# Row means of a 64 MiB tensor: 14-row loads with a shared last part, issued by GpSimd from the third load on

## The chip, the cores and the metric

One core of a Trainium2 chip. The metric is the time of one execution in microseconds (us) on the device; most executions of a kernel agree within 0.3%. All runs compared here were in the fast state, with a granted clock of 1.0. Ratios are the mean time of one kernel's fast runs over the mean of the other's fast runs of the same rounds, so they are not quite the ratios of the medians quoted beside them. The experiments ran in four batches, each on another chip; the kernel before took 164.75, 164.77, 164.87 and 164.93 us there (medians), so a difference of 0.2 us between batches means little.

Words used below: a "row" is 128 x 1024 floats, one row of 1024 for each of the 128 partitions, 0.5 MiB. A load "lands" when its semaphore tells the engines that its data is there. Loads are counted from 0. In the profile DVE is VectorE, ACT is ScalarE, POOL is GpSimd and SP is SyncE; a "packet" is one of its DMA records, here one partition's part of a load.

## The reference

```python
# x: (32, 512, 1024) float32, divisor: 1024.0
def reference(x, divisor):
    return (np.sum(x, axis=-1) / divisor).astype(np.float32)
```

There are 16,384 sums of 1024 numbers. The kernel gives each partition 128 of them, so x is 128 "rows" in the sense above, and all of it is read once.

## The kernel before

SyncE issues every load. VectorE sums the first five rows of a load of eight, ScalarE (ACT) the other three, and the pool has five buffers, so five loads can be under way.

```python
    bulk = [8] * 15
    tail = [4, 2, 1]
    pool = ctx.enter_context(tc.tile_pool(name="bulk", bufs=5))
    # ... (one-off tiles; one PSUM tile that takes ACT's unused output)
    def act_sum(dst, src):
        n = src.shape[-1]
        nc.scalar.activation(junk[:, :n], src, COPY, accum_out=dst)

    def sums(t, j, rows, for_act):
        d = rows - for_act
        if d:
            nc.vector.reduce_sum(out=res[:, j : j + d], in_=t[:, :d, :], axis=AX)
        for r in range(d, rows):
            act_sum(res[:, j + r : j + r + 1], t[:, r, :])

    j = 0
    for rows in bulk:
        t = pool.tile([P, 8, D], F32, name="t")
        nc.sync.dma_start(out=t[:, :rows, :], in_=xr[:, j : j + rows, :])
        sums(t, j, rows, rows * 3 // 8)
        j += rows
    # ... (the tail: loads of 4, 2 and 1 rows; then the last row in three pieces,
    #      two sums of it on VectorE and one on ACT, a sum of the three, two scalings)
    nc.sync.dma_start(out=out_v, in_=res)
```

## Time and profile before

| | before |
|---|---|
| time, median | 164.75 us (164.66 to 164.75, 3 runs) |
| span of the profiled run | 162.9 us |
| DMA engines | at 90% or more in all slices but the first and the last |
| one load of 8 rows | lands every 9.71 us, 432 GB/s |
| VectorE, ACT busy | 53%, 36% |

How to read it: the bytes set the time (the prediction has the sum). An engine's idle time costs nothing here. What can cost something is a moment in which no load is waiting for the DMA engines. The lines of the profile that carry this stand in the prediction.

### The profile page before, as it was taken

The numbers are of one execution on the slowest core, as the hardware profiler recorded it, in microseconds if no ns is written. First come the engines' busy times: TensorE is split into PE (matmuls) and PEld (weight loads), VectorE is DVE, ScalarE is ACT, GpSimd is POOL, SyncE is SP. The second block draws the span as 40 slices with busy tenths as digits, with TensorE's granted clock in tenths as the row PEclk, the third lists the DMA queues.
The fourth block names the chain that finished last, engine by engine and source line by source line (L and its number), as shares of the span: only waits on it lengthen the run. The fifth ranks groups of instructions, "written<-read, shape, count | busy, mean of one in ns | idle before, by whom it ended". The sixth has DMA issues, their size and how long they took to land.

```text
span 162.9 us, 222 instructions
## 1 busy us (share of the span) xinstructions
DVE 87.1 (53%) x22; ACT 58.1 (36%) x101; POOL 0.2 (0%) x4
## 2 busy tenths in 40 slices
DVE  0007639094571917549093672908448092763983
ACT  3006135080531607034080622608043070613692
POOL 0000000000000000000000000000000000000000
DMA  6999999999999999999999999999999999999990
GB/s 209 426 418 443 435 435 435 418 443 435 410 459 426 402 467 435 394 459 435 426 443 418 435 437 418 443 435 410 443 443 402 459 443 410 443 435 398 408 352 16
DMA packets 3169, 67.18 MB, mean 412 GB/s; under 512 B 352, under 2 KB 736, under 8 KB 992
## 3 DMA queue, kind: packets, MB, share of 16 engines
q1 hardware_dynamic: 3168, 67.18, 96.5%
q14 instruction: 1, 0.01, 0.0%
HBM read 67.11 MB, written 0.07 MB: 412 GB/s over the span
## 4 chain that ended last, share of the span: by engine, by line
DMA 90%; DVE 7%; issue 1%; SPq 0%; DVEq 0%
DMA t<-in_x_dram 61%; DMA last<-in_x_dram 30%; DVE res L53 7%; DVE part L77 0%; DVE res L76 0%; DVE part L78 0%; DVE res L79 0%; SPq L60 0%; DVE part L74 0%; DVEq L78 0%
## 5 line engine op out<-in xcount | busy, mean ns | idle before, releaser
L53 DVE TENSOR_REDUCE res<-t 128x5 f32<-128x5120 f32 x15 | 82.3, 5488 | 72.5 <-DMA t<-in_x_dram 72.5
L48 ACT ACTIVATE junk<-t 128x1024 f32<-128x1024 f32 x45 | 46.2, 1027 | 99.2 <-DMA t<-in_x_dram 98.3
L48 ACT ACTIVATION_READ_ACCUMULATOR junk<-t 128x1 f32 x45 | 8.4, 186 | 0.0
L48 ACT ACTIVATE junk<-tail 128x1024 f32<-128x1024 f32 x4 | 4.1, 1028 | 1.7 <-DMA tail<-in_x_dram 1.7
L53 DVE TENSOR_REDUCE res<-tail 128x2 f32<-128x2048 f32 (+1 forms) x2 | 3.4, 1743 | 0.0
L48 ACT ACT_TABLE_LOAD x1 | 1.3, 1283 | 0.7 <-PEq L97 0.7
L74 DVE TENSOR_REDUCE part<-last 128x1 f32<-128x512 f32 x1 | 0.7, 685 | 0.6 <-DMA last<-in_x_dram 0.6
L48 ACT ACTIVATION_READ_ACCUMULATOR junk<-tail 128x1 f32 x4 | 0.7, 186 | 0.0
L77 DVE TENSOR_REDUCE part<-last 128x1 f32<-128x256 f32 x1 | 0.4, 411 | 0.0
L48 ACT ACTIVATE junk<-last 128x256 f32<-128x256 f32 x1 | 0.4, 388 | 0.0
L76 DVE TENSOR_SCALAR res<-res 128x127 f32<-128x127 f32 x1 | 0.2, 216 | 0.0
L78 DVE TENSOR_REDUCE part<-part 128x1 f32<-128x3 f32 x1 | 0.2, 155 | 0.1
L48 ACT ACTIVATION_READ_ACCUMULATOR junk<-last 128x1 f32 x1 | 0.2, 187 | 0.0
L79 DVE TENSOR_SCALAR res<-part 128x1 f32<-128x1 f32 x1 | 0.2, 154 | 0.0
L97 POOL MEMSET const-uint8-127<- 128x1 uint8 x1 | 0.1, 102 | 0.0
L97 POOL MEMSET const-bfloat16-1.0<- 128x1 bf16 x1 | 0.1, 101 | 0.0
L97 POOL MEMSET const-float32-0.0<- 128x1 f32 x1 | 0.1, 98 | 0.2 <-issue 0.2
L97 POOL MEMSET const-float32-1.0<- 128x1 f32 x1 | 0.1, 98 | 0.0
## 6 DMA issues: line engine op xcount, KB each, us to landing
t<-in_x_dram SPq DMA_DIRECT2D x15, 4096.0 KB, 43.0
tail<-in_x_dram SPq DMA_DIRECT2D x1, 2048.0 KB, 47.5
tail<-in_x_dram SPq DMA_DIRECT2D x1, 1024.0 KB, 49.5
tail<-in_x_dram SPq DMA_DIRECT2D x1, 512.0 KB, 50.4
last<-in_x_dram SPq DMA_DIRECT2D x1, 256.0 KB, 48.2
last<-in_x_dram SPq DMA_DIRECT2D x2, 128.0 KB, 34.1
out_dram<-res SPq DMA_DIRECT2D x1, 64.0 KB, 1.5
```

Of the source, the lines that this page charges most:

```text
L48: nc.scalar.activation(junk[:, :n], src, COPY, accum_out=dst)
L53: nc.vector.reduce_sum(out=res[:, j : j + d], in_=t[:, :d, :], axis=AX)
L74: nc.vector.reduce_sum(out=part[:, 0:1], in_=last[:, 0:h], axis=AX)
L76: nc.vector.tensor_scalar_mul(out=res[:, :j], in0=res[:, :j], scalar1=scale)
L77: nc.vector.reduce_sum(out=part[:, 2:3], in_=last[:, h + q : D], axis=AX)
L78: nc.vector.reduce_sum(out=part[:, 3:4], in_=part[:, 0:3], axis=AX)
L79: nc.vector.tensor_scalar_mul(out=res[:, j : j + 1], in0=part[:, 3:4], scalar1=scale)
L97: nc = _bacc.Bacc("TRN2", target_bir_lowering=False, num_devices=1)
```

## The change

Its intent: fewer and larger loads, a shorter end, and loads issued by GpSimd, which has nothing else to do. From the third load on they go through the software descriptor generator, on a queue of their own; loads 0 and 1 stay on SyncE's hardware queue. Three buffers of 14 rows take the place of five of 8. Two smaller edits are left out of the cut below: ACT's unused output gets four PSUM tiles in place of one, and ACT's sums of a load are written ahead of VectorE's.

```diff
-    bulk = [8] * 15
-    tail = [4, 2, 1]
-    pool = ctx.enter_context(tc.tile_pool(name="bulk", bufs=5))
+    bulk = [14] * 8 + [8]
+    split = {14: 6, 8: 4, 4: 2, 2: 1}          # rows for ACT
+    tail = [4, 2]
+    pool = ctx.enter_context(tc.tile_pool(name="bulk", bufs=3))
     ...
-    for rows in bulk:
-        t = pool.tile([P, 8, D], F32, name="t")
-        nc.sync.dma_start(out=t[:, :rows, :], in_=xr[:, j : j + rows, :])
-        sums(t, j, rows, rows * 3 // 8)
+    for i, rows in enumerate(bulk):
+        t = pool.tile([P, 14, D], F32, name="t")
+        tc.keep_in_program_order((nc.sync if i < 2 else nc.gpsimd).dma_start(out=t[:, :rows, :], in_=xr[:, j : j + rows, :]))
+        sums(t, j, rows)
     ...                                          # tail, row and last: nc.gpsimd too
-    (the last row in three pieces, three partial sums, their sum, a scaling)
+    (the last two rows each as 704 + 320 columns, one part on VectorE and one on ACT;
+     one tensor_scalar adds the two parts and scales them)
```

More of the change, by code (lines that the diff above doesn't have):

```diff
@@ L33 @@
     out_v = out.tensor.reshape((P, J)).ap()
-    bulk = [8] * 15
-    tail = [4, 2, 1]
-    assert sum(bulk) + sum(tail) + 1 == J
-    pool = ctx.enter_context(tc.tile_pool(name="bulk", bufs=5))
+    bulk = [14] * 8 + [8]
+    split = {14: 6, 8: 4, 4: 2, 2: 1}
+    tail = [4, 2]
+    assert sum(bulk) + sum(tail) + 2 == J
+    pool = ctx.enter_context(tc.tile_pool(name="bulk", bufs=3))
     one = ctx.enter_context(tc.tile_pool(name="one", bufs=1))
-    psum = ctx.enter_context(tc.tile_pool(name="junk", bufs=1, space=bass.MemoryType.PSUM))
+    psum = ctx.enter_context(tc.tile_pool(name="junk", bufs=4, space=bass.MemoryType.PSUM))
@@ L42, with sums @@
     res = one.tile([P, J], F32, name="res")
     part = one.tile([P, 4], F32, name="part")
-    junk = psum.tile([P, D], F32, name="junk")
     def act_sum(dst, src):
         n = src.shape[-1]
+        junk = psum.tile([P, D], F32, name="junk")
         nc.scalar.activation(junk[:, :n], src, COPY, accum_out=dst)
-    def sums(t, j, rows, for_act):
-        d = rows - for_act
-        if d:
-            nc.vector.reduce_sum(out=res[:, j : j + d], in_=t[:, :d, :], axis=AX)
+    def sums(t, j, rows):
+        d = rows - split[rows]
@@ L54, in sums @@
         for r in range(d, rows):
             act_sum(res[:, j + r : j + r + 1], t[:, r, :])
+        nc.vector.reduce_sum(out=res[:, j : j + d], in_=t[:, :d, :], axis=AX)
     j = 0
-    for rows in bulk:
-        t = pool.tile([P, 8, D], F32, name="t")
-        nc.sync.dma_start(out=t[:, :rows, :], in_=xr[:, j : j + rows, :])
-        sums(t, j, rows, rows * 3 // 8)
+    for i, rows in enumerate(bulk):
+        t = pool.tile([P, 14, D], F32, name="t")
+        tc.keep_in_program_order((nc.sync if i < 2 else nc.gpsimd).dma_start(out=t[:, :rows, :], in_=xr[:, j : j + rows, :]))
+        sums(t, j, rows)
@@ L62 @@
         j += rows
-    for k, rows in enumerate(tail):
-        t = one.tile([P, rows, D], F32, name=f"tail{k}")
-        nc.sync.dma_start(out=t, in_=xr[:, j : j + rows, :])
-        sums(t, j, rows, (rows + 1) // 2)
+    for i, rows in enumerate(tail):
+        t = one.tile([P, rows, D], F32, name=f"tail{i}")
+        tc.keep_in_program_order(nc.gpsimd.dma_start(out=t, in_=xr[:, j : j + rows, :]))
+        sums(t, j, rows)
         j += rows
-    h, q = D // 2, D // 4
-    last = one.tile([P, D], F32, name="last")
@@ L72 @@
-    for a, b in ((0, h), (h, h + q), (h + q, D)):
-        nc.sync.dma_start(out=last[:, a:b], in_=xr[:, j, a:b])
-    nc.vector.reduce_sum(out=part[:, 0:1], in_=last[:, 0:h], axis=AX)
-    act_sum(part[:, 1:2], last[:, h : h + q])
-    nc.vector.tensor_scalar_mul(out=res[:, :j], in0=res[:, :j], scalar1=scale)
-    nc.vector.reduce_sum(out=part[:, 2:3], in_=last[:, h + q : D], axis=AX)
-    nc.vector.reduce_sum(out=part[:, 3:4], in_=part[:, 0:3], axis=AX)
-    nc.vector.tensor_scalar_mul(out=res[:, j : j + 1], in0=part[:, 3:4], scalar1=scale)
@@ L80 @@
-    nc.sync.dma_start(out=out_v, in_=res)
+    c = 704
+    t = one.tile([P, D], F32, name="row")
+    tc.keep_in_program_order(nc.gpsimd.dma_start(out=t, in_=xr[:, j, :]))
+    act_sum(part[:, 0:1], t[:, c:])
+    nc.vector.reduce_sum(out=part[:, 1:2], in_=t[:, :c], axis=AX)
+    nc.vector.tensor_scalar(
+        out=res[:, j : j + 1], in0=part[:, 1:2], scalar1=part[:, 0:1], scalar2=scale, op0=ADD, op1=MULT
+    )
+    nc.vector.tensor_scalar_mul(out=res[:, :j], in0=res[:, :j], scalar1=scale)
@@ new lines @@
+    j += 1
+    t = one.tile([P, D], F32, name="last")
+    tc.keep_in_program_order(nc.gpsimd.dma_start(out=t[:, :c], in_=xr[:, j, :c]))
+    tc.keep_in_program_order(nc.gpsimd.dma_start(out=t[:, c:], in_=xr[:, j, c:]))
+    act_sum(part[:, 2:3], t[:, :c])
+    nc.vector.reduce_sum(out=part[:, 3:4], in_=t[:, c:], axis=AX)
+    nc.vector.tensor_scalar(
+        out=res[:, j : j + 1], in0=part[:, 3:4], scalar1=part[:, 2:3], scalar2=scale, op0=ADD, op1=MULT
+    )
+    tc.keep_in_program_order(nc.sync.dma_start(out=out_v, in_=res))
```

## The prediction

> **What bounds the kernel now.** I read the engines' busy shares first, then the slices, the DMA queues, the chain that ended last, and last the timeline. Shares and slices of the kernel before:
>
> ```profile
> DVE 87.1 (53%) x22; ACT 58.1 (36%) x101; POOL 0.2 (0%) x4
> ...
> DMA  6999999999999999999999999999999999999990
> ...
> q1 hardware_dynamic: 3168, 67.18, 96.5%
> ```
>
> No computing engine is busy for much over half of the span; the DMA engines are at 90% or more in every slice but the first and the last, and one queue does it all for 96.5% of 16 engines' time. The chain (share of the span by what was waited for) says the same:
>
> ```profile
> DMA t<-in_x_dram 61%; DMA last<-in_x_dram 30%; DVE res L53 7%; DVE part L77 0%; DVE res L76 0%; DVE part L78 0%; DVE res L79 0%; SPq L60 0%; DVE part L74 0%; DVEq L78 0%
> ```
>
> 90% is transfers. The 7% of VectorE is where the chain hops from a late-issued load to the reduction that freed its buffer, while other loads were flowing: no idle DMA lies there, as the slices show. The stream's rate is in the timeline (start us, us, what; in brackets the idle time before it):
>
> ```profile
> 100.79 5.49 DVE L53 TENSOR_REDUCE res<-t 128x5 f32<-128x5120 f32 x1 [4.22 <-DMA t<-in_x_dram]
> ...
> 110.50 5.49 DVE L53 TENSOR_REDUCE res<-t 128x5 f32<-128x5120 f32 x1 [4.22 <-DMA t<-in_x_dram]
> ...
> 149.36 5.49 DVE L53 TENSOR_REDUCE res<-t 128x5 f32<-128x5120 f32 x1 [4.22 <-DMA t<-in_x_dram]
> ```
>
> Five loads of 4 MiB land between 100.79 and 149.36, so one takes 9.71 us: 432 GB/s, or 1.214 us a row (a "row" is 128 x 1024 floats, 0.5 MiB). The first load landed at 13.36, which is 3.65 more than its own 9.71. All 128 rows then land by 3.65 + 128 x 1.214 = 159.1; the last piece was issued at 129.9 and landed 29.4 later, at 159.3. So the whole time is the stream, 3.65 in front of it, and what follows it: the last arithmetic ended at 160.34, 1.0 after the landing, then the store and the end, to 162.9 (164.75 as timed).
>
> The first slice is 4.07 us at 209 GB/s, 0.85 MB or 2.0 us of stream. So bytes flow from about 2.1, and some 1.55 of the 3.65 pass between a load's last byte and its semaphore.
>
> **What the Trainium skill says.** (1) "DMA: Bandwidth & Descriptors", Where 436 GB/s comes from: the ports give 435.2 GB/s. The trace agrees, at 432; no way of issuing can gain more than 1% of the stream. (2) The same page, SWDGE vs HWDGE vs iDMA: software and hardware generators feed different queues inside each DMA engine, and the engine takes turns between them. The trace before has one data queue and can't show this; my range depends on it. (3) The same page, Latency and other measured facts: the first byte takes about 1 us on the software path against about 0.6 us. No software load is in this trace. (4) "SBUF — State Buffer", Who interferes with whom: a VectorE reduction never locks GpSimd out on this chip, a tensor_scalar can. The reductions of t are 82.3 us of VectorE here, the tensor_scalars 0.4 us and at the end, when all loads have been issued. So I count no starving of the generator.
>
> **The change part by part.**
>
> *Fewer, larger loads.* Before: 15 loads of 8 rows; after: 8 of 14 and one of 8. If the difference between 9.71 and the 9.64 us that 4 MiB take at the skill's 435.2 GB/s is a cost per load (estimate), six fewer loads, and some fewer small pieces, save about 0.5 us. It is on the path.
>
> *Tail.* Before, 1.0 us of arithmetic followed the landing of the last piece: a reduction (0.41), a sum of three partials (0.155), a scaling (0.154), with waits. After: a 320-wide reduction (between 411 ns for 256 and 685 for 512: 0.48) beside a 704-wide ACT sum started on the earlier piece, and one tensor_scalar (0.15). About 0.75. Saves 0.3.
>
> *More ACT work.* A row costs ACT 1.18 us (starts at 13.38, 14.56, 15.74), VectorE 1.07 ((5488 - 2277)/3). A 14-row load gives ACT 6 x 1.18 = 7.1 us and VectorE 8.70 (5488 + 3 x 1070), and it takes 14 x 1.214 = 17.0 us to arrive. Both stay well ahead: hidden.
>
> *Issuing on GpSimd.* 12 issues, of 1 to 2 us each by (3) (estimate), on an idle engine. The 15 SP issues were no cost either. What counts is only whether a load is in flight when each is issued.
>
> Base, if the DMA engines never run dry: 164.75 - 0.5 - 0.3 = 164.0 us.
>
> *Depth.* Before, five buffers; after, three of 14 rows. In order, a load is issued when the third one back has been consumed, so two loads (34 us) remain: enough, if loads complete in order. **They may not.** Loads 0 and 1 are on the hardware queue, load 2 is the first of the software queue, and its buffer is free, so it goes out at once, beside load 0. Its bytes come before load 1's, but the engines consume load 1 before load 2, and loads 4 and 5 wait for those two.
>
> With equal turns: loads 0 and 2 share the engines from 2.1 to about 36. Load 0 lands at some 36.7, is consumed at 45.4, load 3 has its first byte at 46.9 (1.5 later, estimate). Load 1, alone from 36.1, has 6.2 us left, which shared take 12.4: it ends at 59.3, lands at 60.9, is consumed at 69.6; load 4's first byte is at 71.1. Load 3's last byte comes at 2.1 + 4 x 17.0 = 70.1. So the engines are dry for about 1.0 us; for 2.5 if the issue takes 3 us. After that the two loads in flight are never fewer than one, and order is restored. I take 1.6: **165.6 us**.
>
> **The rivals.**
>
> *No gap (base).* If the engines' turns are a whole load, or favour the hardware queue, load 1 lands by about 54 and load 4 goes out well before 70: 164.0 us. For it: the skill speaks of turns of packets, which can hold many descriptors. Against: in the trace before a packet is one descriptor: 3168 = 22 transfers x (128 + 16), 32 KB each for the large loads.
>
> *Software favoured.* If the software queue gets most turns (longer packets than the hardware's), load 2 ends near 21, load 0 at 36, load 3 passes load 1, and load 1 ends last of the four, at 70.1. Landed at 71.7, consumed at 80.4, load 4 flows from 81.9: the engines are dry for 11.8 us, and the time is about 176. Milder favour gives something between (a 70:30 share 5 to 7 us, by stepping the same schedule: about 170). Nothing in the profile speaks for or against it.
>
> *A slower software stream.* If GpSimd's descriptors cost the engines more, or are cut smaller, 102 of 128 rows suffer: 1% of 124 us is 1.2 us. The software generator as the bound is unlikely: one issue per 17 us, where the trace before shows an issue landing within 12.6 us of which 9.7 are data.
>
> *Hidden anyway* is the issue cost itself in all of these, after the first two loads have put 34 us of data in the queue.
>
> **Range and chances.** I give equal turns with a small gap about half (164.8 to 167), no gap a quarter (163.6 to 164.5), software favoured a fifth (169 to 176), a slower stream the rest (165 to 168). The two limits of 2% are 161.5 and 168.05. Faster than 161.5 would need 3 us less where the stream at its ceiling allows about 1.2: 0.02. Slower: 0.28. Within: 0.70. Range of 8 in 10: 163.6 to 171.
>
> **What would show it.** In the changed kernel's timeline, the first VectorE reduction starts at about 37 (equal turns), about 20 (hardware or whole loads first), or 37 with the second one at 60, 54 or before, or 72 by the same three cases. In the slices, a dip of DMA just after 70 us is the gap, and its depth in us should be the time over 164.0. From 90 on, reductions should start every 17.0 us; 17.2 or more means a slower software stream. A last reduction that ends over 1 us after the last landing would refute the tail. The prediction fails if the software queue takes most turns, if GpSimd needs over 5 us an issue, or if interleaving two queues itself slows the engines.

## The result, and the profile after

| | before | after |
|---|---|---|
| time, median | 164.75 us (164.66 to 165.13, 4 runs) | 165.95 us (165.66 to 166.17, 4 runs) |
| ratio of the fast runs | | 1.0067, 95% interval 1.0043 to 1.0091 |
| span of the profiled run | 162.9 us | 164.3 us |

The change is 0.7% slower, which is within the 2% that counts as the same; 165.6 had been predicted. The page of the changed kernel, for the same lines as before (busy shares, DMA slices, GB/s of each slice, queues):

```profile
DVE 79.1 (48%) x16; ACT 60.9 (37%) x115; POOL 6.7 (4%) x16
...
DMA  6999999999999999969999999999999999999990
GB/s 223 447 447 447 447 447 447 433 405 419 419 391 405 433 447 447 447 223 447 447 447 447 447 421 405 419 433 419 419 405 433 447 447 447 391 439 411 407 391 20
...
q0 software_dynamic: 1568, 52.43, 74.4%
q1 hardware_dynamic: 432, 14.75, 21.3%
```

The engines are no busier, and the bytes are the same. There is one new digit: a 6 in slice 17 (counted from 0; a slice is 4.11 us, so it covers 69.8 to 73.9), where GB/s falls from 447 to 223. Half a slice of stream is lost there, 2.1 us. (The view books a packet whole at its start. The packets start in waves of 16, 2.12 us apart, so a full slice holds two waves and shows 447, above the stream's 433; the size of the hole is read better from the reductions below.) The windows around it, whose last two columns are the DMA share and GB/s, show the same:

```profile
36.00:40.00 4.00, 4.00 (x1) 4.00 (x9) 0.00 (x0) 1.00 1.06 459
40.00:70.00 30.00, 12.85 (x3) 10.44 (x21) 0.53 (x1) 1.00 0.99 428
70.00:74.00 4.00, 4.00 (x1) 4.00 (x9) 0.53 (x1) 1.00 0.69 229
74.00:90.00 16.00, 13.18 (x2) 6.18 (x12) 1.06 (x2) 1.00 1.03 444
```

VectorE's timeline (start, duration; in brackets the idle time before it) shows the order in which the loads came:

```profile
35.47 8.69 DVE L56 TENSOR_REDUCE res<-t 128x8 f32<-128x8192 f32 x1 [35.47 <-DMA t<-in_x_dram]
61.31 25.87 DVE L56 TENSOR_REDUCE res<-t 128x8 f32<-128x8192 f32 x3 [17.15 <-DMA t<-in_x_dram]
90.57 8.69 DVE L56 TENSOR_REDUCE res<-t 128x8 f32<-128x8192 f32 x1 [3.39 <-DMA t<-in_x_dram]
107.48 8.69 DVE L56 TENSOR_REDUCE res<-t 128x8 f32<-128x8192 f32 x1 [8.22 <-DMA t<-in_x_dram]
124.46 8.69 DVE L56 TENSOR_REDUCE res<-t 128x8 f32<-128x8192 f32 x1 [8.30 <-DMA t<-in_x_dram]
```

The first load is ready at 35.47; with one queue for all loads it is ready at 20.61 (first experiment below). The second comes at 61.31, and then three reductions stand back to back ("x3"): loads 2 and 3 had landed by the time load 1 had been summed. And GpSimd's timeline shows when the buffers came free:

```profile
44.73 0.53 POOL L61 DMA_DIRECT2D t<-in_x_dram  x1 [42.81 <-DVE res L56]
70.54 0.53 POOL L61 DMA_DIRECT2D t<-in_x_dram  x1 [25.28 <-DVE res L56]
79.14 0.53 POOL L61 DMA_DIRECT2D t<-in_x_dram  x1 [8.06 <-ACT junk L50]
```

Load 3 goes out at 44.73, load 4 only at 70.54, and at about 70 everything issued before has arrived: four loads of 16.95 us from 2.1 on end at 69.9. The hole at 70 to 72 is what passes between the end of load 1's reduction, at 70.00, which frees the buffer, and the first bytes of load 4.

One view misleads here, the chain that ended last:

```profile
DMA 63%; DVE 23%; another core or an unknown queue 10%; POOL 1%; issue 1%; DVEq 0%; POOLq 0%
```

The 10% are the wait for load 1 (44.16 to 61.28 in the chain by time), which the profile could not put down to a queue. And the hole itself is nowhere in it: the chain follows load 5 back to its issue at 79.14 and takes its 28 us to landing for transfer, part of which was spent in the queue behind load 4. A hole in the stream is to be looked for in the DMA slices.

### The profile page after: what moved, and what is told of

The parts are those of the page before. It is cut to its first block, busy times and chain, and to the rows that moved or that the text cites. A ratio compares the mean times of both kernels' runs of the same rounds, so it can differ in the third digit from the quotient of the medians.

```text
span 164.3 us, 214 instructions
## 1 busy us (share of the span) xinstructions
DVE 79.1 (48%) x16; ACT 60.9 (37%) x115; POOL 6.7 (4%) x16
## 4 chain that ended last, share of the span: by engine, by line
DMA 63%; DVE 23%; another core or an unknown queue 10%; POOL 1%; issue 1%; DVEq 0%; POOLq 0%
DMA t<-in_x_dram 38%; DMA tail<-in_x_dram 25%; DVE res L56 22%; DVE part L75 0%; POOL t L61 0%; POOL tail L66 0%; DVE part L87 0%; DVE res L79 0%; DVE res L88 0%; DVE res L76 0%; POOLq L61 0%; DVEq L88 0%; DVEq L76 0%; DVEq L79 0%
## 5 line engine op out<-in xcount | busy, mean ns | idle before, releaser
L56 DVE TENSOR_REDUCE res<-t 128x8 f32<-128x8192 f32 (+1 forms) x9 | 73.7, 8210 | 81.8 <-DMA t<-in_x_dram 81.8
L50 ACT ACTIVATE junk<-t 128x1024 f32<-128x1024 f32 x52 | 52.4, 1009 | 98.7 <-DMA t<-in_x_dram 98.7
L50 ACT ACTIVATION_READ_ACCUMULATOR junk<-t 128x1 f32 x52 | 9.7, 187 | 0.0
L61 POOL DMA_DIRECT2D t<-in_x_dram x7 | 3.8, 549 | 113.0 <-DVE res L56 96.0
L50 ACT ACTIVATE junk<-tail 128x1024 f32<-128x1024 f32 x3 | 3.1, 1022 | 0.9 <-DMA tail<-in_x_dram 0.9
L66 POOL DMA_DIRECT2D tail<-in_x_dram x2 | 1.0, 527 | 0.0
L50 ACT ACTIVATE junk<-last 128x704 f32<-128x704 f32 x1 | 0.8, 762 | 0.3 <-DMA last<-in_x_dram 0.3
L75 DVE TENSOR_REDUCE part<-row 128x1 f32<-128x704 f32 x1 | 0.9, 878 | 0.0
L84 POOL DMA_DIRECT2D last<-in_x_dram x1 | 0.5, 541 | 0.0
L85 POOL DMA_DIRECT2D last<-in_x_dram x1 | 0.5, 541 | 0.0
L73 POOL DMA_DIRECT2D row<-in_x_dram x1 | 0.5, 527 | 0.0
```

The source lines that it names most:

```text
L61: tc.keep_in_program_order((nc.sync if i < 2 else nc.gpsimd).dma_start(out=t[:, :rows, :], in_=xr[:, j : j + rows, :]))
L66: tc.keep_in_program_order(nc.gpsimd.dma_start(out=t, in_=xr[:, j : j + rows, :]))
L73: tc.keep_in_program_order(nc.gpsimd.dma_start(out=t, in_=xr[:, j, :]))
L75: nc.vector.reduce_sum(out=part[:, 1:2], in_=t[:, :c], axis=AX)
L84: tc.keep_in_program_order(nc.gpsimd.dma_start(out=t[:, :c], in_=xr[:, j, :c]))
L85: tc.keep_in_program_order(nc.gpsimd.dma_start(out=t[:, c:], in_=xr[:, j, c:]))
```

## The experiments

All twelve kernels computed the right result. The theory (A) has two parts. Loads and tail by themselves gain, to about 164.0. The split into two queues makes load 2 travel beside load 0, ahead of load 1, although load 1 is summed first, so that load 4's buffer is free about 2 us too late. The rivals: the larger loads or the tail cost the time (C), or software descriptors do (B). A later form of B, called B' in the expectations, says that load 2 costs as much as it is issued late.

### Every load on SyncE

```diff
-  (nc.sync if i < 2 else nc.gpsimd).dma_start(...)   # and nc.gpsimd for the tail
+  nc.sync.dma_start(...)
```

> The changed kernel with every load issued by SyncE: one hardware queue, same 14-row loads, same tail. Theory A (the 1.2 us come from load 2 going out beside load 0, which leaves the DMA engines dry for some 2.0 us around 71, while loads and tail by themselves gain a little): about 164.0 us (165.95 less 2.0), below the kernel before by 0.7; first VectorE reduction at about 20.6 us (3.65 + 14 x 1.2125), then every 17.0 us; no dip in the DMA slices. Rival C (the larger loads or the new tail are themselves the cost): 165.5 to 166 and no lower than the changed kernel.

Measured: 163.95 us (163.87 to 164.06), ratio 0.9952 (0.994 to 0.9965) to the kernel before. Its slices and reductions:

```profile
DMA  6999999999999999999999999999999999999990
...
20.61 8.69 DVE L56 TENSOR_REDUCE res<-t 128x8 f32<-128x8192 f32 x1 [20.61 <-DMA t<-in_x_dram]
37.52 8.69 DVE L56 TENSOR_REDUCE res<-t 128x8 f32<-128x8192 f32 x1 [8.22 <-DMA t<-in_x_dram]
...
88.36 8.69 DVE L56 TENSOR_REDUCE res<-t 128x8 f32<-128x8192 f32 x1 [8.25 <-DMA t<-in_x_dram]
```

No hole, and loads in order, 16.95 us apart. C falls: larger loads and tail gain 0.8, and the split of the issue costs 2.0. This version beats both kernels. Its fifth reduction at 88.36 is the mark for all that follows: in the changed kernel the fifth starts at 90.57, 2.2 later.

### Every load on GpSimd

```diff
-  (nc.sync if i < 2 else nc.gpsimd).dma_start(...)
+  nc.gpsimd.dma_start(...)
```

> The changed kernel with loads 0 and 1 issued by GpSimd too: one software queue, in order. Theory A: no dry time in the middle, reductions every 17.0 us from the first on; but the first bytes come late by what I take for load 0's head start in the changed kernel (2.2 us: its first reduction came at 35.47 where two loads of equal turns would have landed at 37.65), so the first reduction at about 22.8 and the time 2.2 over the all-SyncE kernel: about 166.2. Rival B (software descriptors slow the stream, about 1.5 us over 102 rows): reductions every 17.2 us or more after the first load. If the head start is no late start but unequal turns, the first reduction comes at 20.6 to 21.3 and the time is 164.0 to 164.7.

Measured: 164.98 us (164.77 to 165.41), ratio 1.0017. Faster than the changed kernel by 1.0, with more software descriptors. No slice after the fifth is under 90%. Its reductions:

```profile
21.73 8.69 DVE L56 TENSOR_REDUCE res<-t 128x8 f32<-128x8192 f32 x1 [21.73 <-DMA t<-in_x_dram]
...
72.96 8.69 DVE L56 TENSOR_REDUCE res<-t 128x8 f32<-128x8192 f32 x1 [8.28 <-DMA t<-in_x_dram]
...
140.70 8.69 DVE L56 TENSOR_REDUCE res<-t 128x8 f32<-128x8192 f32 x1 [8.26 <-DMA t<-in_x_dram]
```

From 72.96 to 140.70 are four loads, 16.94 us each: the software stream is then as fast as the hardware one, and B falls as far as it concerns the rate. (The two steps before, to 38.82 and 55.99, took 17.09 and 17.17; together they are 0.4 over, and I did not follow them up.) My expectation of 166.2 was wrong: the first load is 1.12 late, not 2.2. So a late first byte alone is not the head start that load 0 has in the changed kernel. What it is, the packets tell (below).

### Only load 0 on SyncE

```diff
-  nc.sync if i < 2 else nc.gpsimd
+  nc.sync if i < 1 else nc.gpsimd
```

> Only load 0 on SyncE, loads 1 to the end on GpSimd. Two queues still share the engines at the start, and all but 14 rows are software's, but now the load that shares with load 0 is the next one to be consumed. Theory A: first reduction at 35.5 as in the changed kernel, the second right behind it at 44.2, no dry time around 71, about 164.0 us as with all on SyncE. Rival B (a software stream, or the sharing of the engines itself, costs the time): 165.5 to 166, like the changed kernel.

Measured: 164.21 us (163.96 to 164.32), ratio 0.9964. The two queues still share at the start, and the loss is gone, all but 0.26:

```profile
35.53 17.28 DVE L56 TENSOR_REDUCE res<-t 128x8 f32<-128x8192 f32 x2 [35.53 <-DMA t<-in_x_dram]
54.58 8.69 DVE L56 TENSOR_REDUCE res<-t 128x8 f32<-128x8192 f32 x1 [1.77 <-DMA t<-in_x_dram]
71.52 8.69 DVE L56 TENSOR_REDUCE res<-t 128x8 f32<-128x8192 f32 x1 [8.26 <-DMA t<-in_x_dram]
```

The first load is as late as in the changed kernel (35.53), but the one beside it is the next to be summed. So it is not the sharing of the engines that costs, but who is served ahead of whom.

### What a turn is: the packets of the changed kernel

The DMA view can be narrowed to a stretch. From 5 to 20 us (packets, MB, share of 16 engines):

```profile
q0 software_dynamic: 61, 3.50, 54.1%
q1 hardware_dynamic: 54, 3.10, 47.9%
```

Equal turns, one packet of 56 KB (57,344 bytes, a partition's 14 rows) at a time: 3.50 MB in 61 packets. In narrower stretches they come in waves of 16, one per engine, 2.12 us each (16.95 for 8 packets). Counted from 0 to 6 us, 32 hardware packets start before the first software one: each engine gives load 0 two packets, then takes turns. A load also ends with a small packet for its semaphore, and that too waits for its turn: load 0's last data packets start between 30 and 32, then 16 software packets between 32 and 33, and 15 hardware packets of 0.00 MB are in the stretch from 34 to 35. Two packets ahead less one turn at the end make one packet, 2.12 us. By the reductions it is the same: two loads of equal share would be ready at 20.61 + 16.95 = 37.56, and load 0 was ready at 35.47, 2.1 earlier. I call that the head start h.

From h the loss can be worked out. Let d be what passes between a load's last byte and the first byte of the load that takes its buffer. Load 0 ends at 36 - h, load 3 begins d later, and until then load 1 has the engines to itself, less what load 2 still lacks. Adding up, load 1 ends at 70 + h - d, and load 4 begins at 70 + h. Load 3 ends at 70. So the hole is h. This holds while h is under d / 2; above it, load 3 goes out while load 2 is still running and stands behind it, load 1 shares evenly all the way from 36 - h to its end at 70 - h, and the hole is d - h. In the changed kernel d is 1.55 (last byte to semaphore) + 8.69 (the reduction) + 2.07 (from its end at 70.00 to load 4's first byte, 90.57 - 16.95 - 1.55 = 72.07), 12.3 in all. So the theory claims something odd: a later load 2 must first cost more and then less, and nothing from 12.3 on.

### Load 2 later, by GpSimd memsets ahead of its issue

```diff
+        if i == 2:
+            for _ in range(n):       # n = 4, 5, 7, 9, 11, 13; 0.98 to 1.0 us each
+                tc.keep_in_program_order(nc.gpsimd.memset(scratch, 0.0))   # 128 x 1024
```

> The changed kernel with four GpSimd memsets of 128 x 1024 ahead of load 2's issue, so that load 0 has a longer head start h (read from the run: 37.65 less the first reduction's start; it was 2.2). With equal turns load 1 ends at 70.1 + h - d, where d is what passes from a load's last byte to the first byte of the load that takes its buffer (1.55 + 8.7 + 2.05 = 12.3 by the changed kernel's trace), and load 4's first byte comes at 70.1 + h, when load 3 has ended at 70.1. Theory A: the engines are dry for h while h is under d/2 = 6.1, for 12.3 - h above it, and not at all from h = 12.3 on; the time is 164.0 plus that. So for h = 4, 168.0; for h = 6, 170; for h = 9, 167.3. Rival B (late issue of each software load, or a slower stream, and not the head start): the same time as the changed kernel, 165.95, whatever h.

> Five memsets ahead of load 2 (each 0.98 us from start to start in the run with four). Theory A, now sharper: the two queues take turns of one 56 KB packet per engine, so the head start h of load 0 is a whole number of packets of 16.95 / 8 = 2.12 us (2.1 in the changed kernel, 4.15 with four memsets). Here h = 6.4: first reduction at 31.2. Dry time is the smaller of h and 12.3 - h, so 5.9, and the time is the all-SyncE kernel's 163.95 plus that: 169.9 (170.3 if d is a little longer). Rival B' (a late load 2 costs its lateness, however it comes about): one memset more than the run with four, so 1.0 more than its 168.23: 169.2.

> Seven memsets. Theory A: h = 4 packets = 8.5 us, first reduction at 29.1; now on the falling side: load 3 goes out so early that it stands behind load 2, load 1 ends earlier by each packet of h, and the dry time is 12.3 - 8.5 = 3.8: 167.8 us, less than with five memsets. Rival B' (lateness is the cost): rises on to 171.

> Eleven memsets, so load 2 goes out nearly 11 us later than in the changed kernel. Theory A: h = 6 packets = 12.7 us, first reduction at 24.9; 12.3 - h is under zero, nothing runs dry: 164.0 to 164.3 us, 1.8 faster than the changed kernel that issues load 2 at once, and all loads from the third on are still issued by GpSimd. Rival B': 175.

> Thirteen memsets ahead of load 2, so that load 0 has nearly all its eight packets per engine before load 2 begins. In the run with seven I foresaw four packets and 167.8, and it was 170.61: the packets of its trace show one engine of the 16 switching a packet earlier than the rest, and a load has landed only when its last engine has, so the head start that counted was as with five memsets. With eleven the first reduction came at 27.06, so h = 10.5, and 12.3 - 10.5 = 1.8 was about the loss (2.03). With thirteen: h = 12.7 or more, first reduction at 25 or before, no dry stretch, 164.0 to 164.4 us, though GpSimd still issues all loads from the third on. If one engine again switches a packet early: 165.4 to 166. Rival B' (lateness is the cost): 166 or more.

> Nine memsets, between the runs with seven (170.61) and eleven (165.98). Theory A: h = 8.5 (first reduction near 29.1) and a dry time of 12.3 - 8.5 = 3.8, so 167.8 us; if one of the 16 engines switches a packet early, first reduction near 31.3 and 170. Rival B': no ordering of this kind, a later load 2 is never cheaper.

Measured. "First" is the start of the first reduction, h is 37.56 less that. The "loss by the trace" is how much later than 88.36 the fifth reduction starts, and the "loss by the time" the median less 163.95; "theory" is the smaller of h and 12.3 - h, or 0:

| memsets | first | h | theory | loss by the trace | median | loss by the time |
|---|---|---|---|---|---|---|
| 0 (the changed kernel) | 35.47 | 2.1 | 2.1 | 2.2 | 165.95 | 2.0 |
| 4 | 33.41 | 4.2 | 4.2 | 4.0 | 168.23 | 4.3 |
| 5 | 31.51 | 6.1 | 6.1 | 6.4 | 170.29 | 6.3 |
| 7 | 32.13 | 5.4 | 5.4 | 7.1 | 170.61 | 6.7 |
| 9 | 29.18 | 8.4 | 3.9 | 4.4 | 168.41 | 4.5 |
| 11 | 27.06 | 10.5 | 1.8 | 1.8 | 165.98 | 2.0 |
| 13 | 24.89 | 12.7 | 0 | 0.5 | 164.50 | 0.6 |

The loss rises to above 6 us and falls again to nearly nothing, with the same descriptors by the same generator, and load 2 issued ever later. "Lateness is the cost" (B') falls: with 13 memsets the load goes out 12.5 us later than in the changed kernel (13.73 against 1.25), and the time is 1.45 us shorter. The slices with five and with thirteen memsets, one line of each kernel:

```profile
DMA  6999999999999999509999999999999999899990
```

```profile
DMA  6999999999999999999999899999999998999980
```

With five memsets, half of slice 16 and all of slice 17 (71.6 to 75.8 us) are empty; with thirteen, nothing is missing there. Some later slices are a tenth lower, and the 0.5 us that are left may lie in them; I did not follow them up.

Two rows missed what I had expected by more than 1 us. With seven memsets I had expected four packets' head start and 167.8, and it was 170.61. Of its hardware packets, 79 start before the first software packet, where five per engine would be 80: one engine of 16 changed over a packet earlier. The end of load 0 shows the same: 15 of its 16 completion packets start between 27 and 29 us, the last one between 31 and 32. With eleven memsets I had expected six packets and at most 164.3, and it was 165.98 with five: 14 of load 0's completion packets start between 23 and 25 us, the last two between 26 and 27. A load has landed only when its last engine is done, so one or two engines set h. Given h as it came out, the row with eleven fits the theory. The run with seven was also the least steady (170.10 to 171.35), and its 1.3 to 1.7 us over the theory are not fully explained.

### Packets of half the size on the hardware queue

```diff
-  (nc.sync if i < 2 else nc.gpsimd).dma_start(out=t[:, :rows, :], ...)
+  for a, b in ((0, 7), (7, 14)) if i < 2 else ((0, rows),):
+      (nc.sync if i < 2 else nc.gpsimd).dma_start(out=t[:, a:b, :], ...)
```

> The changed kernel with loads 0 and 1 on SyncE each cut into two of 7 rows, so that the hardware queue's packets are 28 KB and the software queue's stay 56 KB. Same bytes, same order, same queues. Theory A with turns of one packet each: the hardware queue now gets a third of the bytes while both have work; load 2 ends near 28 to 30 us instead of 36, load 0 still near 36 (first reduction 36 to 37.5), load 3 then takes two thirds against load 1, which ends near 62.4 to 63 and is consumed late: second reduction at 64 to 65, dry time 4.6 (equal to 70.1 less what the two-thirds share leaves) to 5.7, 168.5 to 169.7 us. Rival (the engines share by bytes, not by packets): as the changed kernel, first reduction 35.5, 165 to 166.2 us.

Measured: 168.19 us (167.87 to 168.50), ratio 1.0194; fifth reduction at 92.81, 4.45 later than with all loads on SyncE. From 8 to 20 us:

```profile
q0 software_dynamic: 64, 3.67, 70.6%
q1 hardware_dynamic: 56, 1.61, 31.0%
```

Near equal in packets, 70 to 30 in bytes: a turn is a packet, of 28 KB as of 56 KB. The prediction's rival of a software queue with 70% of the bytes, put at about 170, is this case. The rival of sharing by bytes is refuted, and the time is near what the theory gave (168.5 to 169.7), a little under. The first reduction, at 38.31, came later than the 36 to 37.5 expected, and the second, at 63.68, a little before the 64 to 65.

### Two hardware queues and no software descriptors

```diff
+    first = [pool.tile([P, 14, D], F32, name="t") for _ in range(3)]
+    nc.gpsimd.memset(first[2][:, :1, :], 0.0)            # :6 in the second run
+    for i in range(3):
+        eng = nc.scalar if i < 2 else nc.sync            # all later loads: nc.sync
+        tc.keep_in_program_order(eng.dma_start(out=first[i], in_=xr[:, 14 * i : 14 * i + 14, :]))
```

The sums were kept in the order of the loads.

> No software queue at all: loads 0 and 1 on ScalarE's hardware queue, load 2 and the rest on SyncE's, load 2 held back by one 0.98 us GpSimd memset into its own tile so that load 0 goes first, and the sums kept in the order 0, 1, 2. Theory A (two queues and the order they make are the cause, not who writes the descriptors): the same picture as the changed kernel, first reduction at 35.5, second at about 61, DMA engines dry for about 2.1 us near 71, 166.0 us. If load 0's head start should be two packets, 33.4 and 168.2; if load 2 goes first after all, 37.6 and 164. Rival B (software descriptors or their issue cost it): 164.0 us.

> The two hardware queues again, with load 2 held back by a GpSimd memset of six rows of its tile (about 5.8 us) in place of one. Theory A: as in the run with five or six us of delay on the software queue: load 0 has three to four packets per engine to itself at first, first reduction at 31.3 to 31.5, load 4 lands some 6.3 us later than with all loads on SyncE (fifth reduction at about 94.7 against 88.36), 170.2 us. In the run with one row the first reduction came at 36.63 and the loss was 4.36 where A had 2.1. If that excess of 2.3 belongs to two hardware queues as such, it comes on top here: about 172.5. If it was the grid of packets of that run (one engine out of step), 170 to 170.7. Rival B (only software descriptors cost anything): 164.0.

Measured with one row of memset: 168.31 us (167.63 to 168.81), first reduction 36.63, fifth 92.74 (4.4 late). With six rows: 169.35 us (169.25 to 169.61), first reduction 31.29, fifth 93.62 (5.3 late). The second one's slices:

```profile
DMA  6999999999999999547999999999999999899990
```

The hole is there without any software descriptor: two queues suffice, and B is not needed for it. The second run came out 0.85 under the 170.2 expected, and fits in size once its own d is used. The second reduction starts at 65.17 and ends at 73.86, and load 4's first byte comes at 93.62 - 16.95 - 1.55 = 75.12, 1.26 later, where GpSimd took 2.07. So d is 11.5, h is 37.56 - 31.29 = 6.27, and d - h is 5.2, against 5.3 measured. The first run does not fit: h is 0.9 there and the loss 4.4. That it is not in the nature of two hardware queues, the second run shows. The first run's packets show where the excess arose. Load 1, on q10, ends with 16 completion packets: two start before 58 us, twelve between 59 and 62, and two between 63 and 64. From 60 to 61 and from 63 to 64:

```profile
q10 hardware_dynamic: 9, 0.00, 0.5%
...
q10 hardware_dynamic: 2, 0.00, 0.1%
```

By the single packets of the trace the twelve end at 61.01 and the last two start at 63.73, 2.7 us later; load 1 is ready only with these, at 64.12. Without them the loss would have been about 1.7 (an estimate: 4.4 less 2.7), near the 2.1 foreseen. Why two of the engines fell behind stays open.

## Why the prediction was right

**Where the changed kernel stands without the hole.** Predicted 164.0 (0.5 for larger loads, 0.3 for the tail), measured 163.95 with all loads on SyncE. The parts come out a little differently in the trace. Its rows take (139.34 - 20.61) / 98 = 1.2115 us against 1.214, which is 0.3 over 128 rows, not 0.5. Its last piece, issued at 116.6, landed 42.4 later at 159.0, and the last arithmetic ended at 159.83, so 0.8 for 1.0: 0.2 rather than 0.3. The spans differ by 0.6; the medians by 0.8, and the last 0.2 is in neither term. That the base came out within 0.05 is therefore partly luck.

**Which loads share, and which wait.** Predicted with equal turns: load 0 ready at 36.7, load 1 at 60.9, load 3's last byte at 70.1, load 4's first after it. The trace has 35.47, 61.31, a hole from 70 to 72, and order from there on. The turns are equal because the packets are.

**The size of the hole.** This is the term that was off, "1.0 us; for 2.5 if the issue takes 3 us", taken as 1.6; it measured 2.0. I had let load 0 win by about the 1 us of a slower first byte. In truth the first load is 1.1 later (all on GpSimd against all on SyncE), but the engines deal in whole packets of 2.12 us, and h is one of them. The 2.5 was a slip: a slower issue also delays load 3, which leaves load 1 the engines for longer, and by the prediction's own schedule the hole stays at 1.0. So to take 1.6, between 1.0 and 2.5, came nearer to the 2.0 by luck; the order of the loads, the place of the hole and its cause were right by reasoning, with equal turns given about half. (A smaller slip, without effect: 100 rows come through GpSimd, not 102.)

**What would hide.** Issue cost: GpSimd's issues took 0.53 to 0.67 us each, where 1 to 2 had been estimated. Starving of the generator by VectorE, which the Trainium skill ("SBUF — State Buffer", Who interferes with whom) rules out for reductions: none was seen, the issue beside a reduction at 79.14 took 0.53 us like the others. More work for ACT: hidden.

**The rivals.** "Software favoured" did not happen, but could have: with hardware packets of half the size it did, and cost 4.4 us. "No gap" was wrong as a description of this kernel, and is what a different assignment of the same loads gives (164.21). "A slower software stream" is refuted by 16.94 us per load.

## What to carry to other kernels

When loads go out on more than one queue, the order of arrival is no longer the order of issue: the engines dealt packets by turns (61 and 54 in the same 15 us), and a load with a free buffer on the second queue overtakes one that stands in line on the first. With few buffers this can hold back the one load that is needed next; put loads that follow each other on the same queue, or hold back the overtaking one, and size the packets alike. A loss of this kind shows in the DMA slices, not in the chain of waits, and moving the issue to an idle engine gains nothing where the issue was hidden anyway.

## What the Trainium skill lacked or had wrong

- "DMA: Bandwidth & Descriptors", Queues, rings and completion order, and SWDGE vs HWDGE vs iDMA: a packet is described as 4096 bytes or less preferably, typically 9 to 17 descriptors, and as the unit of a turn. Here the unit was a packet of 57,344 bytes, one partition's run, 2.12 us long; 61 software and 54 hardware packets from 5 to 20 us, and 70 to 30 in bytes when the hardware queue's packets were halved.
- The same sections: no figure for how long a load's completion waits behind another queue's packet. Here each of load 0's completion packets came one software packet, about 2.1 us, after its last data.
- The same page, Issuing engines are not separate DMA queues: that spreading loads over engines doesn't help holds, but it can also cost. Here 2.0 us, and up to 6.7 by the moment at which the second queue's first load went out.
- The same page, Measured (HBM→SBUF, 128 partitions, SWDGE, issued from GpSimd): its row of 16 MB in 79.0 us with 425 GB/s does not agree with itself (16 MB in 79.0 us are about 212 GB/s). The runs bear out the rate: 7.34 MB in 16.94 us, 433 GB/s.
- The same page, Latency and other measured facts: about 0.4 us between the first bytes of the two paths. The first load landed 1.12 us later from GpSimd, of which 0.50 is that its issue started at 1.24 instead of 0.74; and a load whose buffer came free began 2.07 us after the reduction's end against 1.26 from SyncE (both worked out from landings).
